# Encoder layer on one core: the moving operands of the sevenfold products placed at other distances from the weights, and one of them cast by itself

## The chip, the cores and the metric

The kernel runs on one core of a Trainium2 chip. The metric is the device time of one execution in microseconds, taken as the median of several runs. One further execution is recorded by the hardware profiler; its views carry the argument.

## What is computed

One layer of an encoder, 512 positions by 1024 channels in float32. Around a mixing part (Fourier mixer and grouped attention) stand two feed-forward halves, and these are what the change touches:

```python
def swiglu(h, w_gate, w_up, w_down):
    return (jax.nn.silu(h @ w_gate) * (h @ w_up)) @ w_down

x = x + 0.5 * swiglu(rms_norm(x, ffn1_norm), ffn1_w_gate, ffn1_w_up, ffn1_w_down)
h = rms_norm(x, mix_norm); u = h @ w_in
f_out = fourier_mixer(u[..., :o0], fnet_w, fnet_b)
a_out = gqa_attention(u[..., o0:o1], u[..., o1:o2], u[..., o2:], q_norm, k_norm)
x = x + jnp.concatenate([f_out, a_out], axis=-1) @ w_out
x = x + 0.5 * swiglu(rms_norm(x, ffn2_norm), ffn2_w_gate, ffn2_w_up, ffn2_w_down)
return rms_norm(x, final_norm)          # d_ff = 2752
```

## The kernel before

**Split numbers.** TensorE works on `fp32r`, a shortened float32. A number is therefore held as a high part (the cast) and a low part (what the cast left over), and a product is taken as high by high, high by low and low by high: three matmuls.

**Groups.** Each feed-forward half (`ffn`, instances 0 and 2) goes through the 2752 inner columns in chunks of 128, in four groups. In the first group every gate and up chunk is a plain product of 24 matmuls (`gate`, line 186: 8 input blocks, three matmuls of 512 columns each). The chunks `c` = 0, 1, ... of that group are called gates here; in the first half, gates 4 to 7 come last. A group's result, `at`, goes through the down weights (`down`, tile `dn`).

**Sevenfold products.** From the second group on, `seven` computes gate and up of one chunk together by seven half-size products instead of eight. Its moving operands are seven parts of the normalised input, made once per half by `operands` and kept in one tile `rt`: `b11`, `b22`, `b21` (blocks of the input itself) and `t1` to `t4` (sums and differences of them). Each part has four blocks of 512 words on a partition: 256 of high part, then 256 of low part. Its stationary operands are weight sums held in slots of the tile `ring`. For each of 35 chunks the order on TensorE is a11 by b11 (bank `r`), a12 by b21 (bank `p`), the previous chunk's a22 by t4 (`r`), s1 by t1 (`q`), s2 by t2 (`r`), s4 by b22 (`q`), s3 by t3 (`r`).

Five of the seven go **by halves**: for each of four blocks, high weights by the high half and by the low half of the moving operand (two matmuls of 256 columns, line 436) and low weights by the high half (one of 256, line 441). The products in `WIDE`, a12 by b21 and s4 by b22, are **merged**: high weights by high and low halves in one matmul of 512 columns (line 432), then low weights by the high half (256 columns, line 441). A merged operand is read "turned", in pieces of four words that step 16 words; the others are read straight on. Every matmul has a weight load of its own, and it runs while the matmul before it streams.

**Where the operands lie.** `PART_AT` gives the words by which each part is shifted; a part itself has 2048 words. In the built program `ring` and `rt` both begin 32 words past a multiple of 64 words, and the weight slots begin 16 words into `ring` (`FRONT`). Modulo 64, the distance from weights to moving operand is thus the part's entry of `PART_AT` less 16. That gives 48 words for b11 and t1 to t4, 32 for b22 and 16 for b21. The products `gate` and `down` are read turned at a distance of 52 (`NEAR`, `LOWER`).

**Making the parts.** For each of four input blocks, `operands` scales two input rows on VectorE into a tile `b` (two buffers), forms four sums `t`, casts the high parts on ScalarE and gets the low parts in one of two ways: by a VectorE subtraction (`lows`, line 130), or by transfer (`rest_by_dma`): ScalarE writes the negated high part to the low part's place (line 159) and GpSimd's queue adds the source to it by a DMA (line 160). Before, b11, b22 and b21 are cast in one instruction of 3 by 256 columns. Gates 5 to 7 of the first half get the low parts of their weights by the same kind of transfer.

The order on TensorE and on SyncE's queue is that of the code; on the other engines a scheduler sets it.

Of the kernel before, what the change touches and what calls it, by code (L numbers as in the profile page):

```python
# [7 lines left out]
F32R = mybir.dt.float32r  # L8
# [5 lines left out]
P = 128  # L14
S = 512
# [11 lines left out]
ROOM = 64  # L27
# [5 lines left out]
GROUPS2 = ((0, "t", 1), range(2, 8), range(8, 14), range(14, 21))  # L33
PLACES = 7
HALF = S // 2
PART_AT = (0, 48, 96, 128, 128, 128, 128)
WIDE = ('a12', 's4')
USES = "a11", "a12", "s1", "s2", "s4", "s3", "a22"
PIECES = (0, 2, 2, 0, 2, 1, 1)
KH = KD // 2  # L40
# [48 lines left out]
def encoder(ctx, tc, A, out):  # L89
# [39 lines left out]
    def lows(lo, src, hi):  # L129
        nc.vector.tensor_tensor(out=lo, in0=src, in1=asf(hi), op=ALU.subtract)  # L130
# [26 lines left out]
    def rest_by_dma(lo, hi, src):  # L157

        nc.scalar.activation(lo, asf(hi), AF.Copy, scale=-1.0)
        nc.gpsimd.dma_start(out=lo, in_=src, accum_op=ALU.add)  # L160
# [123 lines left out]
    def ffn(norm, after, wgu, wd, wdt, groups, opening, closing):  # L284
# [4 lines left out]
        n_ = norm.n  # L289
        n_plain = len(groups[0])  # L290
        with tc.tile_pool(name=f"act{n_}", bufs=1) as ap, tc.tile_pool(name=f"sums{n_}", bufs=2) as sp:
            room(ap, 128)
            acts = ap.tile([P, PLACES * 2 * S + ROOM], F32R, name=f"at{n_}")
            at = acts[:, FRONT + LOWER : FRONT + LOWER + PLACES * 2 * S].rearrange("p (n a b) -> p n a b", a=2, b=S)
            rt = ap.tile([P, 7 * KH * S + PART_AT[-1] + PART_AT[-1] - PART_AT[-2]], F32R, name=f"rt{n_}")
            wt, raws = [], {}
            free, where = list(range(PLACES)), {}

# [33 lines left out]

            begins = [i * KH * S + o for i, o in enumerate(PART_AT)]
            part = {
# [4 lines left out]
            def parts_at(i0, i1, i):  # L339

                step = begins[i0 + 1] - begins[i0] if i1 > i0 + 1 else KH * S
                c = rt[:, begins[i0] : begins[i0] + (i1 - i0) * step].rearrange("p (n r) -> p n r", r=step)
                return (c[:, :, i * S + o * HALF : i * S + (o + 1) * HALF] for o in range(2))

            def operands(rp, i0, i1):
                for i in range(i0, i1):
                    b = sp.tile([P, 4, HALF], F32, tag="raw_g", name=f"b{n_}_{i}")
                    for o, k in ((0, i), (2, i + KH)):
                        nc.vector.scalar_tensor_tensor(
                            out=b[:, o : o + 2].rearrange("p a b -> p (a b)"), in0=x[k],  # L350
                            scalar=gains[:, norm.n, k : k + 1], in1=rp, op0=ALU.mult, op1=ALU.mult,
                        )
                    b12, b11, b22, b21 = (b[:, o] for o in range(4))
                    t = sp.tile([P, 4, HALF], F32, tag=("s12", "s34")[i % 2], bufs=1, name=f"t{n_}_{i}")
                    for o, (p, q) in enumerate(((b12, b11), (b22, t[:, 0]), (b22, b12), (b21, t[:, 1]))):
                        nc.vector.tensor_tensor(out=t[:, o], in0=p, in1=q, op=ALU.subtract)
                    for src, i0, i1 in (b[:, 1:], 0, 3), (t, 3, 7):
                        h, l = parts_at(i0, i1, i)
                        nc.scalar.copy(h, src)
                        if i0 or i < (1 if n_ else 2):  # L360
                            lows(l, src, h)
                        else:
                            rest_by_dma(l, h, src)
# [216 lines left out]
            for gi, group in enumerate(groups):  # L580
                last = gi == len(groups) - 1
                ahead = []
                if gi:
                    rest = seven(range(group[0] + 1, min(group[-1] + 2, NF)), ready)
                else:
                    lent = [acts[:, FRONT + i * KD * P : FRONT + (i + 1) * KD * P] for i in range(PLACES - 4, PLACES)]
                    plain.extend(lent)
                    row = []
                    pss = dict(enumerate(opening(gate, lambda: norm.column([norm.acc]), lambda: row.append(norm.row()))))
                    back(lent[:2])  # L590
                    due, parts, left = [*pss, "t"], list(range(KH)), range(2 * len(pss), 2 * n_plain)
                    pss["t"] = [gate(2 * NF)]
                    tail_weights()
                    for i, c in enumerate(left):
                        pss.setdefault(c // 2, []).append(gate(c, by_dma=i in (1,) if n_ else i > 0))
                        if due:
                            j = due.pop(0)
                            evacuate(at[:, place(j)], n_, pss[j], norm)
                        if c % 2 and c != left[-1]:
                            due.append(c // 2)  # L600
                        while len(parts) * len(left) > (len(left) - 1 - i) * KH:
                            o = parts.pop(0)
                            operands(row[0], o, o + 1)

                    def rest():
                        evacuate(at[:, place(n_plain - 1)], n_, pss[n_plain - 1], norm)
# [167 lines left out]
    with in_order():  # L774
        ffn(n0, n1, A["wgu1"], A["wd1"], A["wdt1"], GROUPS1, opening1, None)
# [667 lines left out]
    with in_order():  # L1443
        ffn(n2, n3, A["wgu2"], A["wd2"], A["wdt2"], GROUPS2, lambda gate, column, row: [[gate(0, {KD - 1: column}), gate(1, {3: row})]], closing)
# [122 lines left out]
```

## Time and profile before

| | us |
|---|---|
| median of 3 runs | 821.11 (819.89 to 821.25) |
| the profiled execution | 820.24 |
| its span, first to last instruction | 818.1 |
| around the span | 2.1 |

| engine | busy us | share of the span |
|---|---|---|
| TensorE, matmuls | 811.6 | 99% |
| TensorE, weight loads | 735.5 | 90% |
| VectorE | 659.9 | 81% |
| ScalarE | 483.9 | 59% |
| GpSimd | 29.3 | 4% |

Matmuls overlap in the pipeline: one of 256 columns is shown as lasting 277 ns, while the next starts some 114 ns after it. What a matmul costs is therefore read from one start to the next, and not from its length. In a timeline, a row with xN is N such instructions in a run.

### The profile page before, as it was taken

The page shows a single profiled execution, that of the slowest core. Times are in us where ns is not written, and L with a number is a line of the kernel's source. Part 1 is how long each engine was busy: PE and PEld are TensorE (multiplying, and loading weights), DVE is VectorE, ACT ScalarE, POOL GpSimd, SP SyncE. Part 2 cuts the span into 40 slices and gives each one's busy share as a digit, 9 for nine tenths or more (in the row PEclk, how much of TensorE's full clock was granted, in tenths as well). Part 3 has the DMA queues.
Part 4 walks back from the last instruction along what each step waited for, and adds up shares of the span by engine and source line. Part 5 has one row for each costly group of instructions (what it writes and reads, how often), then busy time and mean ns, then how long its engine had stood idle before and what let it go on. Part 6 is the DMA issues. An engine that isn't in the chain of part 4 may idle for free.

```text
span 818.1 us, 13082 instructions
## 1 busy us (share of the span) xinstructions
PE 811.6 (99%) x5076; PEld 735.5 (90%) x5076; DVE 659.9 (81%) x1073; ACT 483.9 (59%) x810; POOL 29.3 (4%) x31
## 2 busy tenths in 40 slices
PE   9999999999999999999999999999999999999997
PEld 7888999899989998889998888899988999899987
DVE  7898997489956957799998578999955997489674
ACT  7773664257523735689999448556632674257462
POOL 0110000000000000221000001100000000000001
PEclk9999999999999999999999999999999999999999
DMA  7765322424142313342101235543243332333222
GB/s 258 174 145 175 129 93 72 129 104 143 58 143 82 99 58 117 129 148 66 66 26 53 77 104 135 123 164 120 91 123 111 130 102 66 133 104 97 69 78 103
DMA packets 31565, 89.92 MB, mean 110 GB/s; under 512 B 3728, under 2 KB 9232, under 8 KB 31504
## 3 DMA queue, kind: packets, MB, share of 16 engines
q1 hardware_dynamic: 27776, 82.61, 31.2%
q0 software_dynamic: 3008, 5.51, 3.7%
q10 hardware_dynamic: 720, 0.98, 0.3%
q8 instruction: 39, 0.64, 0.3%
q14 instruction: 22, 0.18, 0.1%
HBM read 84.24 MB, written 2.10 MB: 106 GB/s over the span
## 4 chain that ended last, share of the span: by engine, by line
PE 97%; ACT 1%; DVE 0%; DMA 0%; issue 0%; POOL 0%; POOLq 0%; DVEq 0%; ACTq 0%
PE dn L186 25%; PE r L436 16%; PE mix L186 8%; PE r L441 8%; PE gu L186 8%; PE q L436 4%; PE q L441 4%; PE p L432 4%; PE q L432 4%; PE gu L740 3%; PE p L441 2%; PE mix L1234 2%; PE mix L1200 2%; PE mix L1038 1%; PE mix L1039 1%; PE mix L1040 1%
## 5 line engine op out<-in xcount | busy, mean ns | idle before, releaser
L186 PE MATMUL dn<-at,ring 128*128 128x512 f32 x900 | 202.5, 380 | 0.0
L436 PE MATMUL r<-rt,ring 128*128 128x256 f32 x1120 | 196.9, 277 | 0.0
L186 PEld LDWEIGHTS dn<-at,ring 128*128 128x128 f32 x900 | 168.0, 188 | 28.3
L436 PEld LDWEIGHTS r<-rt,ring 128*128 128x128 f32 x1120 | 169.9, 188 | 3.0
L441 PE MATMUL r<-rt,ring 128*128 128x256 f32 x560 | 154.8, 277 | 0.0
L441 PEld LDWEIGHTS r<-rt,ring 128*128 128x128 f32 x560 | 105.1, 188 | 0.0
L391 ACT CAST ring<-s 128x1024 fp32r<-128x1024 f32 x70 | 73.6, 1051 | 36.9 <-PE r L436 27.5
L575 DVE SCALAR_TENSOR_TENSOR gx<-dn,gx 128x512 f32<-128x512 f32 x61 | 41.8, 688 | 65.6 <-PE dn L186 65.6
L130 DVE TENSOR_TENSOR ring<-s,ring 128x1024 fp32r<-128x1024 f32 x70 | 85.3, 1219 | 7.5 <-ACT ring L391 7.1
L172 ACT CAST ring<-raw_dn 128x768 fp32r<-128x768 f32 (+3 forms) x58 | 45.3, 784 | 71.7 <-PE dn L186 60.4
L441 PE MATMUL q<-rt,ring 128*128 128x256 f32 x280 | 76.9, 275 | 0.0
L130 DVE TENSOR_TENSOR ring<-raw_dn,ring 128x768 fp32r<-128x768 f32 (+3 forms) x58 | 51.5, 891 | 5.8 <-PE r L436 4.4
L441 PEld LDWEIGHTS q<-rt,ring 128*128 128x128 f32 x280 | 52.6, 188 | 0.0
L130 DVE TENSOR_TENSOR ring<-raw_g,ring 128x1024 fp32r<-128x1024 f32 x35 | 42.7, 1219 | 11.0 <-PE p L432 9.6
L436 PE MATMUL q<-rt,ring 128*128 128x256 f32 x280 | 49.5, 276 | 0.0
L432 PE MATMUL p<-rt,ring 128*128 128x512 f32 x140 | 49.3, 386 | 0.0
L186 PE MATMUL gu<-ring 128*128 128x512 f32 x216 | 48.9, 381 | 0.0
L432 PE MATMUL q<-rt,ring 128*128 128x512 f32 x140 | 48.5, 383 | 0.0
L186 PEld LDWEIGHTS gu<-ring 128*128 128x128 f32 x216 | 40.4, 188 | 6.9
L450 ACT COPY u<-r 128x256 f32<-128x256 f32 x70 | 26.1, 373 | 34.6 <-PE r L441 34.3
L391 ACT CAST ring<-raw_g 128x1024 fp32r<-128x1024 f32 x35 | 36.8, 1050 | 14.2 <-DMA raw_g<-in_wgu 10.8
L436 PEld LDWEIGHTS q<-rt,ring 128*128 128x128 f32 x280 | 42.2, 188 | 0.2
(275 smaller groups left out, 1543.2 us busy)
## 6 DMA issues: line engine op xcount, KB each, us to landing
raw_g<-in_wgu SPq DMA_DIRECT2D x35, 512.0 KB, 3.7
raw_u<-in_wgu SPq DMA_DIRECT2D x35, 512.0 KB, 4.4
raw_dn<-in_wd SPq DMA_DIRECT2D x40, 384.0 KB, 3.2
raw_gu<-in_wgu SPq DMA_DIRECT2D x12, 512.0 KB, 3.5
raw_o<-in_wo SPq DMA_DIRECT2D x8, 512.0 KB, 3.4
raw_dn<-in_wd SPq DMA_DIRECT2D x8, 448.0 KB, 3.4
raw_wq<-in_wins SPq DMA_DIRECT2D x4, 512.0 KB, 3.5
raw_f<-in_winf SPq DMA_DIRECT2D x4, 512.0 KB, 3.5
```

The lines of the kernel that those rows point to most:

```text
L130: nc.vector.tensor_tensor(out=lo, in0=src, in1=asf(hi), op=ALU.subtract)
L172: nc.scalar.copy(hi[:, :n, :], raw[:, :n, :])
L186: nc.tensor.matmul(ps, a, b, start=first and b is mhi and a is whi, stop=last and a is wlo)
L391: nc.scalar.copy(hi, src)
L432: nc.tensor.matmul(turned(ps), whi[:, ks], turned(m), start=start, stop=False, skip_group_check=True)
L436: nc.tensor.matmul(ps[:, t], whi[:, ks], m[:, o * HALF :][:, t], start=start and o == 0, stop=False, skip_group_check=True,)
L441: nc.tensor.matmul(o, wlo[:, ks], m, start=False, stop=stop, skip_group_check=True)
L450: nc.scalar.copy(out, ps[:, HALF:] if wide else ps[:, :HALF])
L575: nc.vector.scalar_tensor_tensor(out=x[d][:, t], in0=ps[:, t], scalar=0.5, in1=x[d][:, t], op0=ALU.mult, op1=ALU.add)
L740: nc.tensor.matmul(turned(pss[c]), w[:, k % 2, c], turned(m[k]), start=k == 0 and m is hh and w is hi, stop=k == KD - 1 and w is lo,)
L1200: nc.tensor.transpose(pts[n][:, c * P : (c + 1) * P], prob[t, b, c][:, kc * P : (kc + 1) * P], ident)
L1234: nc.tensor.matmul(turned(outs[t, b]), w, turned(p), start=kc == 0 and i == 0, stop=kc == 3 and i == 1)
```

## The change

`PART_AT` becomes (52, 92, 112, 116, 116, 116, 116). Less 16, modulo 64, that puts b11 and t1 to t4 (the products by halves) at 36 words from the weights instead of 48, b22 at 12 instead of 32, and b21 at 32 instead of 16. The shifts from b11 to b22 to b21 are no longer equal, so one access pattern can't hold the three: b11 is cast by itself, b22 and b21 together. The low part of b11 goes by transfer for all four blocks; those of b22 and b21 by VectorE for block 0 and by transfer for blocks 1 to 3. Before, the first half had blocks 0 and 1 on VectorE and the second half block 0. The tile `rt` keeps its size, and so everything behind it its place.

```diff
-PART_AT = (0, 48, 96, 128, 128, 128, 128)
+PART_AT = (52, 92, 112, 116, 116, 116, 116)
...
-            rt = ap.tile([P, 7 * KH * S + PART_AT[-1] + PART_AT[-1] - PART_AT[-2]], F32R, name=f"rt{n_}")
+            rt = ap.tile([P, 7 * KH * S + -(-PART_AT[-1] // ROOM) * ROOM], F32R, name=f"rt{n_}")
...
-                    for src, i0, i1 in (b[:, 1:], 0, 3), (t, 3, 7):
+                    for src, i0, i1 in (b[:, 1:2], 0, 1), (b[:, 2:], 1, 3), (t, 3, 7):
                         h, l = parts_at(i0, i1, i)
                         nc.scalar.copy(h, src)
-                        if i0 or i < (1 if n_ else 2):
+                        if i0 > 2 or (i0 and i == 0):
                             lows(l, src, h)
                         else:
                             rest_by_dma(l, h, src)
```

TensorE and SyncE have the same instructions in the same order as before; only the addresses in `rt` differ. On ScalarE, in the first half, between the casts of the weights of gates 6 and 7 (`raw_gu_6`, `raw_gu_7`) and the negation that precedes gate 7's transfer (`ACTIVATE ring<-ring`, the second one), there stood before:

```order
L172 CAST ring<-raw_gu_6_441 128x1024
L159 ACTIVATE ring<-ring 128x1024
L663 CAST at_128<-u0p 128x512 x2
L359 CAST rt_129<-t_0_382 128x4x256
L172 CAST ring<-raw_gu_7_493 128x1024
L359 CAST rt_129<-t_1_432 128x4x256
L159 ACTIVATE ring<-ring 128x1024
L172 CAST at_128<-raw_dn_0_0_545 128x384
```

And now, behind gate 6's cast and negation, which still come first:

```order
L359 CAST rt_129<-b_1_432 128x2x256
L663 CAST at_128<-u0p 128x512 x2
L159 ACTIVATE rt_129<-rt_129 128x2x256
L359 CAST rt_129<-t_0_382 128x4x256
L359 CAST rt_129<-t_1_435 128x4x256
L359 CAST rt_129<-b_2_487 128x256
L172 CAST ring<-raw_gu_7_503 128x1024
L159 ACTIVATE rt_129<-rt_129 128x256
L669 ACTIVATE g0p<-u0p 64x512
L359 CAST rt_129<-b_2_487 128x2x256
L172 CAST at_128<-raw_dn_0_0_558 128x384
L159 ACTIVATE ring<-ring 128x1024
```

Gate 7's negation has moved behind seven further instructions: five of the operands of blocks 1 and 2, one Silu and the cast of the first down weights.

On GpSimd's queue, in the first half, there stood before four transfers after the norm's power (`at` and the two of `ring` are the low parts of gates 5, 6 and 7):

```order
L258 TENSOR_TENSOR r_91<-ms_92,mhalf 128x4
L160 DMA at_128<-in_wgu 128x1024
L160 DMA ring<-in_wgu 128x1024 x2
L160 DMA rt_129<-b_2_480 128x3x256
L160 DMA rt_129<-b_3_531 128x3x256
```

And now:

```order
L258 TENSOR_TENSOR r_91<-ms_92,mhalf 128x4
L160 DMA at_128<-in_wgu 128x1024
L160 DMA rt_129<-b_0_379 128x256
L160 DMA rt_129<-b_1_432 128x256
L160 DMA ring<-in_wgu 128x1024
L160 DMA rt_129<-b_1_432 128x2x256
L160 DMA rt_129<-b_2_487 128x256
L160 DMA ring<-in_wgu 128x1024
L160 DMA rt_129<-b_2_487 128x2x256
L160 DMA rt_129<-b_3_541 128x256
L160 DMA rt_129<-b_3_541 128x2x256
```

Four operand transfers now stand ahead of gate 7's, two of them ahead of gate 6's, and seven are issued in place of two. In the second half seven stand in place of three, all behind the one transfer of a gate's weights there.

## The prediction

> **What bounds the kernel now.** I read the page's first parts, then its chain of waits, then who waited for whom on TensorE.
>
> ```profile
> span 818.1 us, 13082 instructions
> PE 811.6 (99%) x5076; PEld 735.5 (90%) x5076; DVE 659.9 (81%) x1073; ACT 483.9 (59%) x810; POOL 29.3 (4%) x31
> PEclk9999999999999999999999999999999999999999
> PE 97%; ACT 1%; DVE 0%; DMA 0%; issue 0%; POOL 0%; POOLq 0%; DVEq 0%; ACTq 0%
> ```
> ```profile
> PE busy L685 <- PEq L1550: 0.8, 1, 0.8
> PE gu L740 <- ACT ring L726: 0.2, 1, 0.2
> ```
>
> TensorE carries 97% of the chain at a full granted clock, and its listed waits come to 1.0 us in all. So the time is the number of matmuls times what passes from one start to the next, and the change touches just that for the matmuls that read `rt`. The groups of matmuls, kept apart by form, give their numbers:
>
> ```profile
> L436 PE MATMUL r<-rt,ring 128*128 128x256 f32 x1120 | 196.9, 277 | 0.0
> L441 PE MATMUL r<-rt,ring 128*128 128x256 f32 x560 | 154.8, 277 | 0.0
> L441 PE MATMUL q<-rt,ring 128*128 128x256 f32 x280 | 76.9, 275 | 0.0
> L436 PE MATMUL q<-rt,ring 128*128 128x256 f32 x280 | 49.5, 276 | 0.0
> L432 PE MATMUL p<-rt,ring 128*128 128x512 f32 x140 | 49.3, 386 | 0.0
> L432 PE MATMUL q<-rt,ring 128*128 128x512 f32 x140 | 48.5, 383 | 0.0
> L441 PE MATMUL p<-rt,ring 128*128 128x256 f32 x140 | 38.5, 275 | 0.0
> ```
>
> By halves go 1120 + 560 + 280 + half of the 280 on bank q, 2100 in all; the other 140 of those are the low-weight matmuls of the merged s4 by b22. The timeline of TensorE shows one round of the seven products; its first column is the start:
>
> ```profile
> 745.29 0.40 PE L436 MATMUL r<-rt,ring 128*128 128x256 f32 x2
> ...
> 746.67 0.39 PE L436 MATMUL q<-rt,ring 128*128 128x256 f32 x2
> ...
> 748.03 0.39 PE L436 MATMUL r<-rt,ring 128*128 128x256 f32 x2
> ...
> 749.39 0.38 PE L432 MATMUL q<-rt,ring 128*128 128x512 f32 x1
> 749.61 0.27 PE L441 MATMUL q<-rt,ring 128*128 128x256 f32 x1
> 749.72 0.38 PE L432 MATMUL q<-rt,ring 128*128 128x512 f32 x1
> 749.94 0.28 PE L441 MATMUL q<-rt,ring 128*128 128x256 f32 x1
> 750.05 0.38 PE L432 MATMUL q<-rt,ring 128*128 128x512 f32 x1
> 750.27 0.27 PE L441 MATMUL q<-rt,ring 128*128 128x256 f32 x1
> 750.39 0.38 PE L432 MATMUL q<-rt,ring 128*128 128x512 f32 x1
> 750.61 0.28 PE L441 MATMUL q<-rt,ring 128*128 128x256 f32 x1
> 750.72 0.40 PE L436 MATMUL r<-rt,ring 128*128 128x256 f32 x2
> ...
> 752.09 0.39 PE L436 MATMUL r<-rt,ring 128*128 128x256 f32 x2
> ...
> 753.45 0.38 PE L432 MATMUL p<-rt,ring 128*128 128x512 f32 x1
> ...
> 754.81 0.40 PE L436 MATMUL r<-rt,ring 128*128 128x256 f32 x2
> ```
>
> A product by halves has 12 matmuls and takes 1.36 to 1.38 us (a22 by t4 1.38, s1 1.36, s2 1.36, s3 1.37, a11 1.36). The merged one on b22, at distance 32, takes 1.33, and the merged one on b21, at distance 16, takes 1.36; both stream the same 3072 columns. Over all 35 rounds, start to start, these are 1.367, 1.338 and 1.361 us: 113.9 ns for a matmul by halves, 334.5 ns for a merged pair at 32 and 340.2 for one at 16. So in the same kind of read the distance costs 5.7 ns a pair. Of the pair at 32, the low-weight matmul (749.61 to 749.72, 749.94 to 750.05, 750.27 to 750.39, 750.61 to 750.72) takes 0.45 us for four, 112.3 ns over all 140.
>
> **The change part by part.** *The products by halves, from 48 to 36 words.* No row shows a straight read at 36. The rows that bound it:
>
> ```profile
> 599.72 11.60 PE L186 MATMUL dn<-at,ring 128*128 128x512 f32 x52
> ```
> ```profile
> 427.79 0.63 PE L1097 MATMUL mix<-pos,near 128*128 128x256 f32 x4
> 428.26 0.38 PE L1234 MATMUL mix<-ph,near 128*128 128x512 f32 x1
> ```
>
> From below: a run of 52 turned matmuls at distance 52 takes (11.60 - 0.38) / 51 = 220.0 ns for 512 columns, 110.0 for 256. From above: four straight reads of 256 columns that in the built program lie at distance 60 take 0.47 us, 117.5 ns each. Between them stand 113.9 (straight, 12 words from the new place) and 112.3 (turned, but 4 words from it). I take 112.3, the row nearest in distance: 2100 x (112.3 - 113.9) = -3.36 us. The ends are 2100 x (110.0 - 113.9) = -8.2 and 2100 x (117.5 - 113.9) = +7.6 us. All of this lies on the path, since TensorE waits for nothing in these stages. The Trainium skill ("TensorE: Matmul & The Clock Gate", Back-to-back issue gap) puts the gap of lone matmuls at N / 2.4 + 2.5 ns, 109.2 ns for 256 columns; by that estimate a read free of any cost would bring -9.9 us, and no run here shows such a row.
>
> *The merged a12 by b21, from 16 to 32.* It takes the place that b22 had: 140 x (334.5 - 340.2) = -0.8 us, with 0 as the poorest end.
>
> *The merged s4 by b22, from 32 to 12.* The nearest row is 16, four words off: 140 x (340.2 - 334.5) = +0.8 us. Ends: 140 x (330.0 - 334.5) = -0.6 by the run at 52, and +2.5 by the 117.5 ns of the row at 60 (a pair is three times 256 columns, 352.5 ns).
>
> *ScalarE, VectorE and the transfers.* Each block now has two casts where it had one, and b11 a negation; VectorE loses one subtraction. All this falls into the first group's gates, and the one cover that gets thin is that of gate 7's low weights in the first half. Its rows are those of TensorE, of ScalarE, and of GpSimd's queue with the time to landing:
>
> ```profile
> 44.09 10.72 PE L186 MATMUL gu<-ring 128*128 128x512 f32 x48
> ```
> ```profile
> 38.78 1.05 ACT L172 CAST ring<-raw_gu 128x1024 fp32r<-128x1024 f32 x1
> ...
> 40.68 1.05 ACT L159 ACTIVATE ring<-ring 128x1024 fp32r<-128x1024 f32 x1
> 41.64 0.50 ACT L172 CAST at<-raw_dn 128x384 fp32r<-128x384 f32 x1
> 42.04 0.83 ACT L359 CAST rt<-b 128x768 fp32r<-128x768 f32 x1
> 42.90 0.63 ACT L669 ACTIVATE g0p<-u0p 64x512 f32<-64x512 f32 x1
> ```
> ```profile
> 42.03 0.86 POOL L160 DMA_DIRECT2D ring<-in_wgu  x1 [5.18 <-ACT ring L159]
> ```
> ```profile
> DMA to landing us min/median/max: 5.4/5.4/5.4
> ```
>
> Gates 6 and 7 are the 48 matmuls from 44.09, 220 ns apart. Gate 7 begins at 49.4, and its third matmul, the first on low weights, at 49.8. The transfer is issued at 42.03 and lands at 47.4, so 2.4 us are spare. Now seven instructions stand ahead of the negation that did not: the Silu (0.63), the down cast (0.50), and five on operands of 256 or 512 elements, which by the casts of 384 (0.50) and 768 (0.83) cost about 0.4 and 0.6, 2.6 together. That is 3.7 us, less about 0.8 that ScalarE stood idle there and 0.1 for each instruction by which neighbours overlap in the timeline: 2.2 to 2.9. The landing slips to between 49.6 and 50.3, up to 0.5 us late, and four transfers of operands now stand ahead of it on GpSimd's queue. I take 0.3 us, with ends of 0 and 1.5.
>
> VectorE gains a wait. A buffer of `b` is free only when the transfers out of it have landed, so the scaling of block 3 waits for block 1's. Behind it on VectorE stand the sums of the last blocks, the low parts of the first down weights and the results of gates 4 and 5; the first down product starts at 54.7 and wants these last at about 56. A wait of a microsecond is covered there by some 3 us. The parts themselves are wanted only when the sevenfold products start, at 74.0 in the first half. In the second half the one gate that gets its low weights by transfer stands ahead of all operands on the queue, so I cost that at nothing.
>
> *Sum.* -3.36 - 0.80 + 0.80 + 0.30 = -3.06 us. The profiled execution took 820.24, 2.1 of it around the span, so it would take 817.2. The median of the runs shown lies 0.87 above that execution, and the forecast is to stand beside the median: 821.11 - 3.06 = 818.1 us.
>
> **The rivals.**
>
> *Straight reads dislike 36 (slower).* In the round above, the two products by halves that follow merged ones begin at 0.40 for their first pair where the others show 0.39, and take 1.38 and 1.37 instead of 1.36. So at 48 a straight read has a settled state and a dearer one that it falls into after a disturbance. If 36 never reaches the settled state, every matmul by halves costs what the row at 60 shows: +7.6 - 0.8 + 0.8 + 0.3 = +7.9 us, 829.0. It decides from 114.5 ns a matmul on (0.6 x 2100 = 1.3 us, and the 0.3 of gate 7). Half way, at 115.7 ns, it gives 825.2. Against it speaks only that the nearest read by distance is a quick one. Straight reads are quick in this trace at 48 alone, which is a good reason to keep it at 0.37.
>
> *The distance does not matter to straight reads (no change).* Settled, a matmul by halves takes 1.36 / 12 = 113.3 ns. The run at 52 takes 220.0 for twice the columns, 106.7 more. So both are 106.7 ns for each 256 columns and 6.6 ns on top, and a fixed cost of a matmul would look like this. Then the merged products cancel and gate 7 leaves +0.3: 821.4 us. The Trainium skill ("TensorE: Matmul & The Clock Gate", Step-by-step: what each phase is for) goes further: weights and moving operand have read ports of their own, and loading weights takes nothing from the running matmul. By that rule the trace should show no difference between the pairs at 16 and 32, and it shows 5.7 ns. I give this case 0.15.
>
> *36 is free of the cost (faster still).* At the lower end, 110.0 ns, it is -8.2 + 0.3 = -7.9, 813.2 us. Nothing but a turned read shows such a pace: 0.08.
>
> That the distances do not change as said can be left out: `rt` keeps its size and start, and in the built program all 2660 matmuls on it read at 36, 32 or 12.
>
> **How the numbers follow.** The forecast has 0.40. Its own range runs from 111.2 ns a matmul (-5.4) to 113.0 (-1.6), 815.7 to 819.5 us. About 0.2%, 1.6 us, is what a measurement of this kernel can tell from no change. Faster: 0.40 + 0.08 = 0.48. Same: 0.15. Slower: 0.37. The range must take in most of the slower case: 814.5 leaves out most of the 0.08, and 827.5, 116.8 ns a matmul by halves, leaves out the upper third of the 0.37.
>
> **What would show it.** In the timeline of the changed kernel a product by halves should take 1.35 us (12 x 112.3 ns), the one on bank p 1.34 and the merged one on bank q 1.36. From 1.38 us on for those by halves the rival is right; at 1.36 to 1.37 the distance is nothing to them. Gate 7's third matmul should start within 0.5 us of the second, and its transfer land near 50 us. A new wait of TensorE between 55 and 74 us, or at about 530, would say that the operands' handling was not covered.

## The result and the profile after

The changed kernel takes 835.29 us (833.85 to 836.67) where the kernel before, on the same chip, takes 820.93 (819.89 to 821.25): a ratio of 1.0177, 95% interval 1.0157 to 1.0197. The forecast was 818.1 us with a range of 814.5 to 827.5: the measured time lies above both.

The page and the list of what TensorE waited for show two things at once: 10.0 us more of busy TensorE, and two waits that were not there.

```profile
span 833.9 us, 13137 instructions
PE 821.6 (99%) x5076; PEld 744.0 (89%) x5076; DVE 661.0 (79%) x1072; ACT 486.9 (58%) x827; POOL 37.3 (4%) x40
PE 87%; DVE 5%; issue 2%; DMA 2%; ACT 2%; POOL 1%; POOLq 0%; DVEq 0%; ACTq 0%; SPq 0%
```
```profile
PE gu L186 <- DMA ring<-in_wgu: 2.9, 1, 2.9
PE dn L186 <- DVE at L130: 1.9, 1, 1.9
```

**The reads.** TensorE's timeline of one round, with the first row of each product (a11, a12 by b21, a22 by t4, s1, s2, s4 by b22, s3, the next a11):

```profile
756.98 0.40 PE L436 MATMUL r<-rt,ring 128*128 128x256 f32 x2
...
758.38 0.39 PE L432 MATMUL p<-rt,ring 128*128 128x512 f32 x1
...
759.73 0.40 PE L436 MATMUL r<-rt,ring 128*128 128x256 f32 x2
...
761.15 0.40 PE L436 MATMUL q<-rt,ring 128*128 128x256 f32 x2
...
762.57 0.40 PE L436 MATMUL r<-rt,ring 128*128 128x256 f32 x2
...
764.00 0.38 PE L432 MATMUL q<-rt,ring 128*128 128x512 f32 x1
...
765.33 0.39 PE L436 MATMUL r<-rt,ring 128*128 128x256 f32 x2
...
766.73 0.40 PE L436 MATMUL r<-rt,ring 128*128 128x256 f32 x2
```

The products by halves take 1.40 to 1.43 us where they took 1.36 to 1.38, and the first pair of each shows 0.40. Start to start over all 35 rounds, a11 and s3 take 1.403 and 1.397 us, a22, s1 and s2 1.423, 1.422 and 1.422. That is 117.8 ns a matmul instead of 113.9: 2100 x 3.9 = 8.2 us. The merged pair at 12 takes 334.4 ns (before, at 32: 334.5), the one at 32 takes 338.1 (before, at 16: 340.2), which is -0.3 us.

**Gate 7.** TensorE, and then ScalarE and GpSimd's queue around the same place; the bracket is the idle time ahead and what ended it:

```profile
43.50 5.90 PE L186 MATMUL gu<-ring 128*128 128x512 f32 x26
52.34 6.58 PE L186 MATMUL gu<-ring 128*128 128x512 f32 x22 [2.95 <-DMA ring<-in_wgu]
```
```profile
44.43 0.62 ACT L359 CAST rt<-b 128x512 fp32r<-128x512 f32 x1 [3.18 <-DMA rt<-b]
44.95 0.51 ACT L172 CAST at<-raw_dn 128x384 fp32r<-128x384 f32 x1
45.37 1.05 ACT L159 ACTIVATE ring<-ring 128x1024 fp32r<-128x1024 f32 x1
...
53.63 0.62 ACT L359 CAST rt<-b 128x512 fp32r<-128x512 f32 x1 [3.61 <-DMA rt<-b]
```
```profile
37.43 1.21 POOL L160 DMA_DIRECT2D rt<-b  x1 [1.22 <-ACT rt L159]
...
46.72 0.86 POOL L160 DMA_DIRECT2D ring<-in_wgu  x1 [4.93 <-DVE t L356]
```

ScalarE stands idle for 3.2 us ahead of block 2's cast of b22 and b21, until the transfer of the low parts of block 1's b22 and b21, issued at 37.43, has landed at about 44.4. Two instructions behind that cast is gate 7's negation. So gate 7's transfer is issued at 46.72 instead of 42.03, its low weights are there at 52.3, and the third matmul of gate 7 starts 3.3 us after the second. Then the granted clock is down. These are the windows after this wait and after the one in the second half, with the granted clock (PEclk) behind the five busy times:

```profile
52.34:55.30 2.96, 2.96 (x7) 2.38 (x8) 0.67 (x2) 1.61 (x3) 0.09 (x1) 0.50 0.69 107
...
541.53:546.00 4.47, 4.47 (x20) 3.67 (x21) 4.47 (x8) 2.40 (x5) 0.00 (x0) 1.00 0.77 251
```

At a clock of 0.50 some seven matmuls of gate 7 start 427 ns apart: on average the 22 from 52.34 take (6.58 - 0.38) / 21 = 295 ns each instead of 220, 1.6 us more. The wait and the slow clock cost 3.1 + 1.6 = 4.7 us.

**The second half.** The same cast of blocks 2 and 3 waits there too, and a down product is late:

```profile
517.51 0.62 ACT L359 CAST rt<-b 128x512 fp32r<-128x512 f32 x1 [1.28 <-DMA rt<-b]
...
524.09 0.62 ACT L359 CAST rt<-b 128x512 fp32r<-128x512 f32 x1 [1.70 <-DMA rt<-b]
```

The late product is the wait of 1.9 us in the list above; its matmul starts at 541.53. From start to start this gap costs 2.2 us beyond a matmul's 220 ns, two smaller ones near it 0.4; one at 71.1 us costs 0.4 more. All in all 8.2 - 0.3 + 4.7 + 2.6 + 0.4 = 15.6 us, and the span grew by 833.9 - 818.1 = 15.8. The nearness of the two is in part chance: TensorE is 0.6 us ahead of the trace before when it comes to gate 7, and 0.7 us of the growth lie behind the last matmul.

### The profile page after: what moved, and what is told of

The parts are those of the page before. It is cut to its first block, busy times and chain, and to the rows that moved or that the text cites. A ratio compares the mean times of both kernels' runs of the same rounds, so it can differ in the third digit from the quotient of the medians.

```text
span 833.9 us, 13137 instructions
## 1 busy us (share of the span) xinstructions
PE 821.6 (99%) x5076; PEld 744.0 (89%) x5076; DVE 661.0 (79%) x1072; ACT 486.9 (58%) x827; POOL 37.3 (4%) x40
## 4 chain that ended last, share of the span: by engine, by line
PE 87%; DVE 5%; issue 2%; DMA 2%; ACT 2%; POOL 1%; POOLq 0%; DVEq 0%; ACTq 0%; SPq 0%
PE dn L186 23%; PE r L436 16%; PE r L441 8%; PE mix L186 6%; PE q L436 4%; PE q L441 4%; PE p L432 4%; PE q L432 4%; PE gu L186 3%; PE gu L740 3%; PE p L441 2%; PE mix L1234 2%; PE mix L1200 2%; PE mix L1038 1%; PE mix L1039 1%
## 5 line engine op out<-in xcount | busy, mean ns | idle before, releaser
L436 PE MATMUL r<-rt,ring 128*128 128x256 f32 x1120 | 202.4, 280 | 0.0
L441 PE MATMUL r<-rt,ring 128*128 128x256 f32 x560 | 156.8, 280 | 0.0
L441 PE MATMUL q<-rt,ring 128*128 128x256 f32 x280 | 77.4, 276 | 0.0
L186 PE MATMUL gu<-ring 128*128 128x512 f32 x216 | 50.6, 390 | 2.9 <-DMA ring<-in_wgu 2.9
L130 DVE TENSOR_TENSOR ring<-raw_g,ring 128x1024 fp32r<-128x1024 f32 x35 | 42.7, 1221 | 11.5 <-PE p L432 9.6
L436 PE MATMUL q<-rt,ring 128*128 128x256 f32 x280 | 51.4, 280 | 0.0
L391 ACT CAST ring<-raw_g 128x1024 fp32r<-128x1024 f32 x35 | 36.7, 1049 | 15.6 <-DMA raw_g<-in_wgu 10.1
```

Source lines behind the costliest of these rows:

```text
L186: nc.tensor.matmul(ps, a, b, start=first and b is mhi and a is whi, stop=last and a is wlo)
L391: nc.scalar.copy(hi, src)
L436: nc.tensor.matmul(ps[:, t], whi[:, ks], m[:, o * HALF :][:, t], start=start and o == 0, stop=False, skip_group_check=True,)
L441: nc.tensor.matmul(o, wlo[:, ks], m, start=False, stop=stop, skip_group_check=True)
```

## The experiments

Theory A says that placement and handling each add their part; B that the placement is everything and the waits follow from it; C that the handling is everything; D that the merged products' new distances, and not 36, upset the matmuls behind them. The first four runs share a kernel before of 822.53 us, the next four one of 821.84, the last four, single runs, one of 820.05. A distance is always that from the weights, modulo 64 words.

**The handling alone.** The kernel before with the last two hunks of the change (the split casts and more transfers), and `PART_AT` left at (0, 48, 96, 128, 128, 128, 128).

> The placement of before (48, 32, 16 words), with the split casts and the transfers of the change. Theory A (two causes that add up, the read at 36 words and waits for transfers): about 828 us, matmuls by halves back at 113.9 ns, gate 7's low weights about 3 us late and TensorE at half pace for some 1.5 us after it, and a wait in the second half's down products as in the changed kernel. Rival B (placement is everything, the waits only follow from slower matmuls): 821 to 822 us. Rival C (the handling is everything, and the matmuls got longer because transfers and ScalarE disturb them): 834 to 836 us, with 117 to 118 ns for the matmuls by halves.

Measured: 822.34 us, ratio 1.0003 (0.9989 to 1.0017). Neither the 4.7 us at gate 7 nor the slow reads are there (114.0 ns a matmul by halves; here and below a wait of up to 0.9 us for ScalarE, at the end of a product or two, is left out of the pace). The time is B's, not A's 828 nor C's. GpSimd's queue has gate 7's transfer where it was before the change, and TensorE goes through gate 7 without a break:

```profile
42.04 0.86 POOL L160 DMA_DIRECT2D ring<-in_wgu  x1 [0.61 <-ACT ring L159]
```
```profile
45.74 9.18 PE L186 MATMUL gu<-ring 128*128 128x512 f32 x41
```

So C falls, and so does A's sum. But all the casts and transfers of the change are in this kernel, so the waits need something of the placement too.

**The shift alone.** The kernel before with other entries, which need no split cast (and the changed kernel's line for the size of `rt`):

```diff
-PART_AT = (0, 48, 96, 128, 128, 128, 128)
+PART_AT = (52, 100, 148, 180, 180, 180, 180)
```

> The handling of before, one cast of three parts and its transfers, with all parts shifted by the same 52 words: products by halves at 36 words from the weights, the merged ones at 20 (b22) and 4 (b21). Theory A: matmuls by halves at 117.8 ns as in the changed kernel, no new wait, so about 829 us plus what the merged pairs do at 20 and 4 (0 to 2 us). Rival C: 113.9 ns and 821 to 823 us. Rival D (not 36 but the merged products' new distances 12 and 32 unsettle the matmuls behind them): 113.9 ns at 36 here, unless 20 and 4 unsettle them too.

Measured: 831.91 us, ratio 1.0118 (1.0085 to 1.0151). The matmuls by halves, at 36, take 118.1 ns; no new wait of the operands. The reads alone cost some 9 us. Since b22 now lies at 20 and b21 at 4, this can't tell 36 from D.

**The changed kernel without its transfers.** All low parts by VectorE:

```diff
-                        if i0 > 2 or (i0 and i == 0):
+                        if True:
```

> The placement and split casts of the change, with the low parts of b11, b22 and b21 all by VectorE and none by transfer. Theory A: the waits go and the slow reads stay, 117.8 ns by halves, 828 to 829 us. Rival C: 113.9 ns, 821 us. If VectorE, with some 5 us more work in each half, becomes late for the first down products, there is a wait of up to 2 us at that place.

Measured: 834.5 us, ratio 1.0145 (1.0114 to 1.0176). The reads stay as after the change (117.8 ns). Gate 7's wait is gone, and VectorE's extra subtractions are late elsewhere instead:

```profile
PE dn L186 <- DVE at L130: 2.7, 2, 1.7
PE dn L186 <- DVE ring L130: 1.8, 1, 1.8
```

So this run doesn't price the waits; it swaps them, and its time is above the 828 to 829 us expected.

**48 words kept, the merged products at 12 and 32.** As the last kernel (all low parts by VectorE), with

```diff
-PART_AT = (52, 92, 112, 116, 116, 116, 116)
+PART_AT = (0, 92, 112, 128, 128, 128, 128)
```

> Products by halves left at 48 words, the merged ones at the distances of the change (b22 12, b21 32), split casts, all low parts by VectorE. Theory A: 113.9 ns by halves, the merged pairs on b21 quicker by up to 5.7 ns, so 820 to 821 us. Rival D: the matmuls behind the merged products stay at 117 to 118 ns, 828 us.

Measured: 832.98 us, ratio 1.0129 (1.0098 to 1.0161), and the matmuls by halves, whose addresses are those of before, take 117.2 ns, some 7 us. D is right in part; the time is above its 828 us since the waits for VectorE of the last kernel are here too (3.0 us). The timeline shows where the pace changes. These are the first rows of s1, s2, s4 by b22 (at 12), s3 and the next a11, in the first round behind a down product:

```profile
79.71 0.40 PE L436 MATMUL q<-rt,ring 128*128 128x256 f32 x2
...
81.08 0.39 PE L436 MATMUL r<-rt,ring 128*128 128x256 f32 x2
...
82.44 0.40 PE L432 MATMUL q<-rt,ring 128*128 128x512 f32 x1
...
83.80 0.40 PE L436 MATMUL r<-rt,ring 128*128 128x256 f32 x2
...
85.21 0.40 PE L436 MATMUL r<-rt,ring 128*128 128x256 f32 x2
```

Up to the merged product at 12 a product by halves takes 1.37 and 1.36 us; behind it 1.41 (83.80 to 85.21), and so on until the next down product, although each further round has the merged product at 32 (a12 by b21) in it.

**The step of 20 words alone.** Between b22 and b21 the change has a step of 20 words (92 to 112), the handling alone had 48. In the built program's order on ScalarE (not a trace) the rows of the cast name what it waits for; of the changed kernel, and of the handling alone:

```
L359 CAST rt_129<-b_2_487 128x2x256 [waits DMASW4_49]
L359 CAST rt_129<-b_2_487 128x2x256 [waits DVE_49]
```

DMASW is a transfer of GpSimd's queue, here that of the low parts of block 1's b22 and b21. In programs with steps of 16, 32, 48 or 64 words the cast waits for VectorE only, in those with a step of 20 for the transfer. Built with other steps, the program has the wait for the transfer at 4, 12, 28, 36, 44 and 52 words and not at 8, 24 and 40, so it is multiples of 8 that are free of it, and not only those of 16, as the expectation has it. The cast and that transfer write different words. This kernel has the changed kernel's handling and

```diff
-PART_AT = (52, 92, 112, 116, 116, 116, 116)
+PART_AT = (0, 48, 68, 128, 128, 128, 128)
```

> PART_AT is (0, 48, 68, 128, 128, 128, 128) with the handling of the change: by halves at 48 words and b22 at 32 as before, b21 at 52, so that the step from b22 to b21 is 20 words, as in the changed kernel, where the run with the handling alone had 48. Theory S (the waits come from the 20-word step: in the built program the cast of a block's b22 and b21 waits for the block before's transfer as soon as the step is no multiple of 16 words): gate 7's low weights come about 3 us late again and TensorE runs at half pace after it, the second half's first down product waits 2 to 3 us, +5 to +8 us in all, 826 to 829 us, with matmuls by halves at 113.9 ns. Rival H (they come from the slower matmuls' timing or from the placement, not the step): no new wait, 821 to 823 us. Rival D (a merged product away from 32 and 16 unsettles the matmuls behind it): halves near 117.5 ns, +7.5 us more.

Measured: 833.88 us, ratio 1.0147 (1.0124 to 1.0170). The waits are back, with halves at 48:

```profile
PE gu L186 <- DMA ring<-in_wgu: 1.9, 1, 1.9
PE dn L186 <- DVE at L130: 1.9, 1, 1.9
```
```profile
ACT rt L359 <- DMA rt<-b: 8.8, 4, 4.7
```

Theory S holds, at its upper end: the clock drops behind both waits, and each costs about 3.8 us. The rest is mostly D's: b21, now at 52, slows the products behind it. The timeline shows a11, a12 by b21, s1, s2, s4 by b22 (at 32), s3 and the next a11:

```profile
77.67 0.39 PE L436 MATMUL r<-rt,ring 128*128 128x256 f32 x2
...
79.04 0.38 PE L432 MATMUL p<-rt,ring 128*128 128x512 f32 x1
...
80.42 0.40 PE L436 MATMUL q<-rt,ring 128*128 128x256 f32 x2
...
81.84 0.40 PE L436 MATMUL r<-rt,ring 128*128 128x256 f32 x2
...
83.25 0.38 PE L432 MATMUL q<-rt,ring 128*128 128x512 f32 x1
...
84.59 0.41 PE L436 MATMUL r<-rt,ring 128*128 128x256 f32 x2
...
85.97 0.39 PE L436 MATMUL r<-rt,ring 128*128 128x256 f32 x2
```

The same reads at 48 take 1.37 us, then 1.42 and 1.41 behind the merged product at 52, and 1.38 again behind the one at 32. Over 35 rounds a11 takes 1.361, s1 1.414 and s2 1.413 us.

**The changed kernel with a step of 16 words.** Only b21 is moved, from 32 to 28:

```diff
-PART_AT = (52, 92, 112, 116, 116, 116, 116)
+PART_AT = (52, 92, 108, 116, 116, 116, 116)
```

> PART_AT is (52, 92, 108, 116, 116, 116, 116) with the handling of the change: by halves at 36 and b22 at 12 as in the changed kernel, b21 at 28 in place of 32, so that the step is 16 words. Theory S: gate 7's wait and the second half's waits are gone (each below 0.5 us), the slow reads stay at 117.5 to 118 ns: 821 + 8 = 829 us, 827.5 to 830.5. Rival H: the waits stay, 834 to 836 us.

Measured: 831.66 us, ratio 1.0117 (1.0096 to 1.0137). Gates 6 and 7 run through, and of the second half's wait 0.3 us are left:

```profile
44.32 10.72 PE L186 MATMUL gu<-ring 128*128 128x512 f32 x48
```

The reads are slow as before (118.3 ns). Theory S again. The time is 1 us above the range given, since the halves came 0.5 ns slower yet (1.1 us) and the pair at 28 costs 342.6 ns.

**36 words, the merged products as before.** With the changed kernel's handling,

```diff
-PART_AT = (52, 92, 112, 116, 116, 116, 116)
+PART_AT = (52, 112, 160, 180, 180, 180, 180)
```

> PART_AT is (52, 112, 160, 180, 180, 180, 180) with the handling of the change: by halves at 36 words, the merged products at 32 and 16 as before, step 48. Theory T (straight reads at 36 have no quick pace, whatever runs ahead of them): 117 to 118 ns a matmul by halves, 828 to 830 us. Rival D (at 36 they would be as quick as at 48, and it is the merged product at 12, 20 or 4 that unsettles them): 113 to 114.5 ns, 820 to 823 us.

Measured: 830.6 us, ratio 1.0110 (1.0086 to 1.0134), 117.9 ns. So 36 does its harm without the merged products' new distances. The products a22 that stand by themselves between down products, six in every kernel, show it with no merged product ahead of them. This is the first row of one and that of the down product behind it, before the change and in the changed kernel:

```profile
133.73 0.39 PE L436 MATMUL r<-rt,ring 128*128 128x256 f32 x2
...
135.09 0.38 PE L186 MATMUL dn<-at,ring 128*128 128x512 f32 x1
```
```profile
139.61 0.40 PE L436 MATMUL r<-rt,ring 128*128 128x256 f32 x2
...
141.03 0.39 PE L186 MATMUL dn<-at,ring 128*128 128x512 f32 x1
```

That is 1.36 and 1.42 us, and it is so for all six in every kernel here with 48 and with 36. But "no quick pace", as theory T had it, is too strong. These are s1, s2 and the start of s4 in one round, then a22 by t4 and s1 (with the start of the next product between two dots) in the following one:

```profile
76.74 0.40 PE L436 MATMUL q<-rt,ring 128*128 128x256 f32 x2
...
78.17 0.40 PE L436 MATMUL r<-rt,ring 128*128 128x256 f32 x2
...
79.59 0.38 PE L432 MATMUL q<-rt,ring 128*128 128x512 f32 x1
...
85.10 0.39 PE L436 MATMUL r<-rt,ring 128*128 128x256 f32 x2
...
86.47 0.39 PE L436 MATMUL q<-rt,ring 128*128 128x256 f32 x2
```

The same s1 and s2 take 1.43 and 1.42 us, and one round later a22 by t4 takes 1.37, its matmuls 113 and 114 ns apart. At 36, too, both paces occur; here the slow one is the rule.

**48 words, both merged products at 32.** The part of the change that was to help, with its handling:

```diff
-PART_AT = (52, 92, 112, 116, 116, 116, 116)
+PART_AT = (0, 48, 112, 128, 128, 128, 128)
```

> PART_AT is (0, 48, 112, 128, 128, 128, 128) with the handling of the change: by halves at 48 words as before, both merged products at 32, step 64. The part of the change that should help, alone: 140 pairs of a12 by b21 become 5.7 ns cheaper, -0.8 us; the matmuls by halves stay at 113.9 ns, or come to 113.6 if the product at 16 unsettles them too. Theory S with D: no new wait, 820.0 to 822.5 us, 0.998 to 1.001 of the kernel before. Rival: the two merged products at the same distance unsettle something else, over 824 us.

Measured: 822.5 us, ratio 1.0008 (0.9992 to 1.0024). The pair with b21 costs 333.6 ns instead of 340.2, -0.9 us, the halves stay at 113.8, and no wait that TensorE's list adds is over 0.6 us. It is no faster than the kernel before by anything that was measured; no version here beats it.

**Four other distances for the halves.** Both merged products at 32, so that they set out alike.

> PART_AT is (4, 48, 112, 132, 132, 132, 132) with the handling of the change: by halves at 52 words, where turned reads cost 110.0 ns a 256 columns; both merged products at 32, as in all four runs of this scan, so that these alone set which pace the matmuls behind them begin with. Theory N (the prediction's reading: the pace goes with the distance, near by near): 110 to 113 ns. Theory Q (straight reads have a quick and a slow pace, and a merged product at 32 puts them into the quick one whatever their own distance): 113 to 114 ns. Rival R (each distance has its own pace for straight reads, and 48 is the only quick one tried): over 115 ns, 825 us and more.

> PART_AT is (60, 112, 176, 188, 188, 188, 188): by halves at 44 words, both merged products at 32. Theory N: between 48 and 36, 113.5 to 117 ns. Theory Q: 113 to 114 ns. Rival R: 116 to 119 ns as at 36, 827 to 832 us.

> PART_AT is (48, 112, 176, 176, 176, 176, 176): everything at 32 words. Theory N: 111.5 to 113 ns, as the merged product there, 817 to 820 us. Theory Q: 113 to 114 ns, 820 to 823 us. Rival R: 116 to 119 ns, 827 to 832 us. If it is under 113.0 ns it is the quickest version so far.

> PART_AT is (32, 48, 112, 160, 160, 160, 160): by halves at 16 words, both merged products at 32. Theory N: 113.4 ns, as the merged product at 16. Theory Q: 113 to 114 ns, 820 to 823 us. Rival R: 116 to 119 ns, 827 to 832 us.

| by halves at | 48 | 16 | 36 (merged at 32, 16) | 32 | 44 | 52 |
|---|---|---|---|---|---|---|
| us | 822.5 | 830.84 | 830.6 | 832.91 | 833.52 | 832.32 |
| ns a matmul | 113.8 | 117.7 | 117.9 | 118.6 | 119.2 | 119.3 |
| us for a22 by itself | 1.36 | 1.41 | 1.42 | 1.43 | 1.43 | 1.44 |

Rival R: of the six distances 48 alone is quick as a rule. Near distances are no guide (44 is as poor as 52), and neither is the pace of turned reads: at 52 they cost 110.0 ns a 256 columns in the gates and the straight ones 119.3.

## Why the prediction was wrong

*The products by halves (forecast 112.3 ns, -3.4 us).* This step failed first. It took the price of the nearest row by distance, a turned read at 32, for a straight read at 36. It was 117.8 ns and +8.2 us. The 36-alone run shows that the distance itself does it, and the scan that a turned row says nothing of a straight one. The rival "straight reads dislike 36" had it, with 117.5 ns from a straight read at 60. Its reason, that straight reads are quick in the trace at 48 alone, was the better argument and was given 0.37. Even so the rival's time, 829.0, falls short by 6.3 us, since it kept the forecast's waits.

*The merged products (forecast -0.8 and +0.8).* They came to -0.3 and 0.0. The sizes are small, but the step missed a cost: what a merged product does to the products behind it. With the halves at 48 and 12 for b22 the halves lose 3.3 ns each (117.2), 7 us. The round that the forecast read shows a slow pace of a few matmuls only, but the trace before has a longer one. At 285.65 us the first matmul of a merged product at 32 takes 0.33 us to the next instead of 0.22, and the six products by halves behind it take 1.41 us each, through merged ones at 16 and 32, until the next down product. This is s1, with the start of s2:

```profile
292.70 0.40 PE L436 MATMUL q<-rt,ring 128*128 128x256 f32 x2
...
294.11 0.40 PE L436 MATMUL r<-rt,ring 128*128 128x256 f32 x2
```

So 117.7 ns a matmul, 0.2 from the rival's price, stood in the trace before at the old distance.

*Gate 7 (forecast +0.3, ends 0 and 1.5).* It cost 4.7 us. The step counted seven instructions ahead of the negation and summed their lengths, 2.2 to 2.9 us. The trace has 4.7 us between the old and the new issue of the transfer, and the difference comes from the wait of the cast of block 2, which the order's rows, read without their waits, don't show. The negation's new place was itself a sign: with the same casts and transfers and no wait, in the handling alone, it keeps its old one. The slow clock behind the wait (1.6 us) was not in the sum either.

*The second half (forecast 0).* It cost 2.6 us by the same wait. The reason given, that the gate's transfer stands ahead of all operands on the queue, was true and beside the point: the late work was on ScalarE and VectorE. With the 16-word step a listed wait of 0.3 us is left of 1.9. That the cast's wait makes the down product late is shown by the two kernels with and without the 20-word step; the path from one to the other was not followed.

*VectorE's wait for block 3's buffer (forecast covered).* Right in the handling alone, where it is 0.5 us and TensorE's list has 0.2 us behind VectorE in all. In the changed kernel such waits are three, 3.2 us together; what they cost beside the cast's wait was not priced.

*The rivals.* "The distance does not matter to straight reads" is refuted by every run at another distance. The Trainium skill ("TensorE: Matmul & The Clock Gate", Step-by-step: what each phase is for) says that loading the next weights takes no read bandwidth from the running matmul. By that rule the run with 48 kept and 12 and 32, in which weights, banks and the halves' addresses are those of before, should show the halves at 113.9 ns, and it shows 117.2. So the rule does not give the time here. What passes the pace from one product to the next was not found.

*The sum.* The profiled execution took 835.71 us, the forecast for it was 817.2. Of the 18.5 us between, 11.5 are the halves (8.2 + 3.4), 4.4 gate 7, 2.6 the second half and 0.4 the gap at 71 us; the merged products take back 0.3.

## What to carry to other kernels

Where operands are placed to a pattern, price a new place by a row of the same kind of read at the same place, and where there is none, take the poorest such row, not the nearest. Read a moved instruction's waits along with its order: a scheduler that moves one back has often been given a new wait, and a new stride in an access pattern can be what gave it. A merged or turned read is to be judged by what it leaves to the matmuls behind it, not by its own pace alone.

## What the runs showed of the hardware

- Matmuls by halves have more than one settled pace for the same instructions and addresses: 113.4 and 117.7 ns at 48 words, 113.4 and up to 118.7 at 36. In the rounds shown the pace changes behind merged products. At 48, one at 12 or 52 leaves the slow pace; one at 32 brings back the quick pace in the 20-word run, and does not in the run with 12 and 32, nor in the six slow products of the trace before. Why was not settled.
- A short wait can halve the clock. The Trainium skill ("TensorE: Matmul & The Clock Gate", What's actually happening) has the clock at half after an idle window of about 3.4 us and notes that the window runs free. In the 20-word run the windows behind the two waits, listed at 1.9 us each, have a mean granted clock of 0.63 and 0.61:

```profile
51.47:55.40 3.93, 3.93 (x11) 3.14 (x12) 0.02 (x1) 2.54 (x5) 1.04 (x1) 0.63 0.46 138
...
539.70:543.60 3.90, 3.90 (x12) 3.08 (x12) 3.90 (x8) 2.06 (x4) 0.00 (x0) 0.61 0.77 246
```

  Eight or so matmuls there start 427 ns apart, for 3.4 us, from about a microsecond after the wait is over; the equal wait of 1.9 us at 541.5 of the changed kernel left the clock at 1.00. So less idle time than the Trainium skill's window was enough, and not each time. That the window runs free may be why; no run here shows it.
- The adding transfers of GpSimd's queue land late, in the changed kernel's first half (its line 160, 36 to 57 us) 4.7 to 7.7 us after issue; ScalarE's casts that wait for one stand idle for 3.2 and 3.6 us there:

```profile
DMA to landing us min/median/max: 4.7/5.8/7.7
```
